# Two queues of side work in a streaming-encoder block, and all expert gate tables made beside the dense up products

## The chip, the cores and the metric

The kernel runs on one core of a Trainium2 chip, in one launch. The metric is device time in microseconds (us), the median over runs. The engines are PE (TensorE; PEld is its loading of weights), DVE (VectorE), ACT (ScalarE), POOL (GpSimd, which here issues the gathers) and SP (SyncE, which issues all other transfers). They run side by side, each in the order of its own program, and wait for each other on semaphores.

## What is computed

One layer over 1024 tokens of width 1024, in float32. What matters here:

```python
hn = rms_norm(h, norm_mix_w)
proj = hn @ w_in                                  # z, x/B/C, dt, GLU, branch gates
y_ssm = ssd_chunked_scan(...) + d_skip[:, None] * x_ssm        # 32 heads of 64
y_a = gated_group_rms_norm(y_ssm, z, ssd_norm_w) @ w_ssd_out
y_b = silu(layer_norm(causal_depthwise_conv(u, conv_dw_w))) @ w_conv_out
h = h + (sigmoid(gate_a) * y_a + sigmoid(gate_b) * y_b) @ w_o
# PEER: 8 heads, each picks 16 of 128*128 experts for each token
sv, si = lax.top_k(scores, 16)                    # of 128 keys, twice per head
best, j = lax.top_k(cand, 16)                     # of the 16*16 sums
gate = softmax(best)
act = gelu(einsum("thkd,td->thk", u_tab[expert], xb))
h = h + einsum("thk,thkd->td", gate * act, v_tab[expert])
h = h + sigmoid(rms_norm(h) @ w_ple_gate) * (p @ w_ple_proj)
return rms_norm(h, final_norm_w)
```

A token needs 128 experts; each has a row of 1024 numbers in `u_tab` (`peer_u`) and in `v_tab` (`peer_v`).

## The kernel before

The tokens are worked in two halves of 512. Each matmul in float32 is made of three in a rounded type: `weight` loads 128x1024 numbers of a weight ("a weight" below), ACT makes its high part `hl` (L156) and DVE the rest (L157), and `mm3` makes 8 x 3 matmuls of 128x512. In order the stages are glu (16 weights), gates0 (17), ssd0 (48), merge0 (32), choose0 (16), the same four again for the second half (gates1 to choose1), and then the expert layer.

The expert layer handles its tokens in two ways. The second quarter and the fourth (512 tokens) go through all 16384 experts densely: `dense_up` multiplies a weight of `peer_ut` with the tokens (128 experts, index e) and takes the GELU, `dense_down` multiplies that by the gate G of each token for each expert, and by a weight of `peer_v`. G is nearly all zeros and is built by `gate_table`: for four tokens DVE makes a one-hot tile in a `row` buffer (L734, L736), PE multiplies it (L739, "a set" below) and ACT copies it out (L742); a piece of CT tokens is then written to `DG` in DRAM. There are four tables of 128 tokens, one for each block that goes the dense way.

The first and the third quarter are gathered, in four blocks of 128 tokens numbered 0 to 3. `gather_up` fetches 128 rows of `peer_u` for each of 128 steps (`fetch`, L763: an indirect DMA of 512 KB into one of eight `row` buffers) and DVE multiplies them with the tokens and adds up (L778, "a product"). `gather_down` fetches rows of `peer_v`, four tiles for each of 32 steps ("a sum step"), and PE adds them up in `gv` (L797). Which experts a token needs comes from `choose` (the first top-k) and `choose_block` (the second), both on DVE.

The e's are split. In the stage up, the first EU = 56 of them are multiplied and `z` is parked in DRAM (`DZ`); in both, the other 72 go through up and down at once, in groups of four; in down, the 56 parked ones are read back. finish ends the layer: f1 for the dense tokens, f0 for the gathered.

Choosing, gathering, tables and the wide convolution are written as generators that give up after a bit of work and name its price. Each `weight` calls `tick`, which runs them as far as a credit goes that the stage's entry in `rates` gives:

```python
    def tick(self, anchor):
        with self.tc.issue_after(anchor.ins):
            self.cc = self.run(self.cq, self.cc + self.cr)
            self.gc = self.run(self.gq, self.gc + self.gr)
```

`cq` holds the convolution, `gq` all the rest, one after the other or woven (`weave(a, b, n)`: after each part of a, n parts of b). What an engine then does first is set by the order in which a scheduler places the recorded instructions; every engine keeps to it.

Of the kernel before, what the change touches and what calls it, by code (L numbers as in the profile page):

```python
# [8 lines left out]
F32 = mybir.dt.float32  # L9
# [12 lines left out]
S = 1024  # L22
# [7 lines left out]
CT = 16  # L30
# [6 lines left out]
for _name, _w in (("nm", 8), ("cw", 128), ("cb", 32), ("sn", 16), ("dw", 248), ("db", 8), ("lw", 8),  # L37
                  ("lb", 8), ("bo", 8), ("nf", 8), ("np", 8), ("fn", 8)):
    PCOL[_name] = (_n, _w)
    _n += _w  # L40
# [3 lines left out]
class K:  # L44
    def begin(k):
        xs = [k.xin(h) for h in range(2)]
        hn = [k.norm_in(0, xs[0])]
        with k.tc.issue_after(k.rx.ins):
            hn.append(k.norm_in(1, xs[1]))
        for j in range(2):  # L50
            k.nc.sync.dma_start(k.dsk[64 * j:64 * j + 64], k.I["dsk"][j::2].partition_broadcast(64))
        k.stage("glu")
        for i in range(8):
            k.glu_in(i, hn)
            k.cq.append(k.conv31(0, i))
        k.cq.extend([k.conv31(1, i) for i in range(8)])
        k.hn = hn[0]

    def mix(k, h):
        k.stage(f"gates{h}")  # L60
        k.ssd_dt(h)
        for i in range(16):
            k.gates_in(h, i)
        k.stage(f"ssd{h}")
        for g in range(NG):
            k.ssd_group(h, g)
        k.stage(f"merge{h}")
        if h:
            k.gq = deque([k.weave(chain(k.gate_table(0), k.gate_table(1)), chain(*k.gq), 1)])
        k.merge(h)  # L70

    def __init__(self, ctx, nc, tc, I, out):
        self.nc, self.tc, self.I, self.out = nc, tc, I, out
        self.sb = ctx.enter_context(tc.tile_pool(name="sb", bufs=1))
        self.ps = ctx.enter_context(tc.tile_pool(name="ps", bufs=1, space=PSUM))
        self.dr = ctx.enter_context(tc.tile_pool(name="dr", bufs=1, space=DRAM))
        self.scope = self.gp = None
        self.bufs = {"A": 15, "F": 8, "U": 9, "cu": 1, "ca": 1}
        self.EU, self.G4 = 56, 4
        self.cq, self.gq = deque(), deque()  # L80
        self.cc = self.gc = 0.0
# [9 lines left out]
    def run(q, credit):  # L91
        while q and credit > 0:
            try:
                credit -= next(q[0])
# [12 lines left out]
    def tick(self, anchor):  # L107
        with self.tc.issue_after(anchor.ins):
            self.cc = self.run(self.cq, self.cc + self.cr)
            self.gc = self.run(self.gq, self.gc + self.gr)  # L110

    def flush(self, q):
        self.run(q, 1e9)

    def stage(self, name):
        self.cr, self.gr = self.rates[name]


    def A(self, shape, dtype=F32, tag="A", pool=None):
        t = (pool or (self.ap if tag == "A" else self.scope)).tile(  # L120
            [128, {"cu": 544, "F": 516}.get(tag, 512)], F32, name=tag, tag=tag, bufs=self.bufs[tag])
# [79 lines left out]
    def setup(self):  # L201
# [6 lines left out]
        self.dsk = c([128, 16], "dsk")  # L208
# [230 lines left out]
    def ssd_pair(self, h, u, X, z, C, G):  # L439
# [66 lines left out]
        nc.vector.scalar_tensor_tensor(X, X, self.dsk[:, u:u + 1], pd, op0=OP.mult, op1=OP.add)  # L506
# [218 lines left out]
    def gate_table(self, i):  # L725
# [3 lines left out]
        for c in range(NC):  # L729
            st = [self.A([128, 32, CT], tag="F") for _ in range(4)]  # L730
            for q in range(CT // 4):
# [4 lines left out]
                nc.vector.tensor_tensor(oh[:, 1], oh[:, 1], wt[:, t0:t0 + 4, None].to_broadcast([128, 4, 128]), op=OP.mult)  # L736
                p = self.sp()
# [6 lines left out]
                yield 1.9  # L744
# [4 lines left out]
    def gather_setup(self, blk):  # L749
        h, b = blk  # L750
# [8 lines left out]
        blk += [ix, gt, act]  # L759
# [7 lines left out]
    def gather_up(self, blk):  # L767

        self.gather_setup(blk)
        h, b, ix, gt, act = blk  # L770
# [10 lines left out]
        nc.vector.tensor_tensor(act, act, gt, op=OP.mult)  # L781

    def gather_down(self, blk):

        h, b, ix, gt, act = blk
        nc = self.nc
        po = self.ps.tile([128, 2, 512], F32, name="gv", tag="gv", bufs=1)
        for s in range(32):
# [14 lines left out]
            yield 4.0  # L803
# [15 lines left out]

    def gather(self, h, bs):  # L820
        blks = [[h, b] for b in bs]
        for blk in blks:
            yield from self.gather_up(blk)
        for blk in blks:
            yield from self.gather_down(blk)
# [114 lines left out]
def body(nc, tc, I, out):  # L940
    with ExitStack() as ctx:
# [5 lines left out]
        with tc.tile_pool(name="mid", bufs=1) as k.scope:  # L947
            k.begin()
            for h in range(2):
# [4 lines left out]
                if h == 0:  # L954
                    k.hn = [k.split(k.load(k.Dhn[i])) for i in range(KT)]
                    bl = [[h, b] for b in range(HB)]
                    up, down = [k.gather_up(x) for x in bl], [k.gather_down(x) for x in bl]
                    k.gq.extend([cb[0], up[0], k.weave(down[0], chain(*cb[1:], up[1]), 3), down[1]])
        k.stage("up")
        with tc.tile_pool(name="up", bufs=1) as k.scope:  # L960
            bl = [[1, b] for b in range(HB)]
            up, down = [k.gather_up(x) for x in bl], [k.gather_down(x) for x in bl]
            rest = chain(*k.gq)
# [9 lines left out]
        with tc.tile_pool(name="A2", bufs=1) as k.ap, tc.tile_pool(name="end", bufs=1) as k.scope:  # L973
# [9 lines left out]
            k.flush(k.gq)  # L983
# [11 lines left out]
def layouts(x, p, norm_mix_w, w_in, conv_ssd_w, conv_ssd_b, dt_bias, a_log, d_skip, ssd_norm_w, w_ssd_out,  # L995
# [16 lines left out]
    def vec(a):  # L1012
# [10 lines left out]
        vec(norm_ple_w[0]), vec(final_norm_w)], axis=1)  # L1023
# [4 lines left out]
        "hpar": c(np.stack([A(dt_bias[0]), A(a_log[0])], axis=1)), "dsk": c(A(d_skip[0])),  # L1028
# [25 lines left out]
```

## Time and profile before

| | |
|---|---|
| median of 3 runs | 4177.55 us (4168.93 to 4183.31) |
| the profiled execution | 4178.62 us; its span from first to last instruction 4176.8 us |
| busy in the span | PE 3735.2 us (89%), DVE 3122.0 (75%), ACT 1477.6 (35%), POOL 1331.2 (32%) |
| moved by DMA | 1030.48 MB, mean 247 GB/s |
| granted TensorE clock, mean | 0.945 of full speed |

Busy times are those of one profiled execution. A matmul's end is modelled and matmuls overlap, so a busy PE need not be at its peak. POOL is counted busy while it issues a fetch; the transfer itself shows in the DMA columns, whose share is that of all 16 DMA engines. 1 MB is a million bytes.

### The profile page before, as it was taken

What the parts mean: (1) busy time and instruction counts of PE and PEld (TensorE: products, weight loads), DVE (VectorE), ACT (ScalarE), POOL (GpSimd) and SP (SyncE); (2) the same over time, 40 slices, a digit from 0 to 9 for tenths busy, and PEclk for the clock granted to TensorE, in tenths of its full rate; (3) what the DMA queues carried; (4) which work ended last, traced back from release to release, by engine and by line L of the source; (5) the groups of instructions that cost most, each with busy time, mean ns of one, the idle gap of its engine ahead of it and who ended that gap; (6) DMA issues with size and microseconds to landing.
All of it is one profiled execution on the core that took longest, in us unless ns stands there. A gap on an engine that the chain in (4) does not pass through costs nothing. (4 is left out here: it accounts for less than half of the span.)

```text
span 4176.8 us, 50925 instructions
## 1 busy us (share of the span) xinstructions
PE 3735.2 (89%) x17772; PEld 2825.4 (68%) x17772; DVE 3122.0 (75%) x5917; ACT 1477.6 (35%) x2616; POOL 1331.2 (32%) x1087
## 2 busy tenths in 40 slices
PE   7999898899974798899868988988999999899977
PEld 5887776678763476677745567777777777667646
DVE  5888888989899888789898347877855555764445
ACT  3135566343332355454412224422222222222233
POOL 0000000000266634244463430255644444433330
PEclk9999999999986899999979999999999999999988
DMA  3243234443698967689997884889999999999872
GB/s 135 89 154 109 95 109 132 152 145 111 223 334 302 331 233 265 237 297 346 320 312 262 315 297 152 281 290 311 338 327 318 314 309 312 325 334 316 302 253 81
DMA packets 479457, 1030.48 MB, mean 247 GB/s; under 512 B 177184, under 2 KB 208032, under 8 KB 479200
## 3 DMA queue, kind: packets, MB, share of 16 engines
q0 software_dynamic: 147456, 536.94, 35.7%
q1 hardware_dynamic: 331744, 490.29, 35.6%
q8 instruction: 140, 2.29, 0.2%
q14 instruction: 117, 0.96, 0.1%
HBM read 935.19 MB, written 91.88 MB: 246 GB/s over the span
## 5 line engine op out<-in xcount | busy, mean ns | idle before, releaser
L763 POOL DMA_INDIRECT row<-in_peer_u_dram,ix x512 | 699.1, 1366 | 1158.4 <-DMA ix<-Didx 410.5
L763 POOL DMA_INDIRECT row<-in_peer_v_dram,ix x512 | 625.0, 1221 | 837.2 <-PE gv L797 454.9
L173 PE MATMUL mm<-xk,hl 128*128 128x512 f32 x2000 | 811.3, 409 | 62.7 <-ACT F L363 22.8
L174 PE MATMUL mm<-xk,hl 128*128 128x512 f32 x2000 | 804.5, 404 | 9.7 <-DVE xk L165 9.7
L778 DVE SCALAR_TENSOR_TENSOR row<-row,xr 128x1024 f32<-128x1024 f32 x512 | 612.3, 1221 | 130.3 <-DMA row<-in_peer_u_dram,ix 118.1
L157 DVE TENSOR_TENSOR hl<-raw,hl 128x1024 fp32r<-128x1024 f32 x422 | 514.7, 1222 | 214.5 <-ACT hl L156 209.2
L156 ACT ACTIVATE hl<-raw 128x1024 fp32r<-128x1024 f32 x422 | 444.3, 1054 | 622.4 <-PE mm L176 288.8
L176 PE MATMUL mm<-xk,hl 128*128 128x512 f32 x2000 | 513.5, 394 | 3.4 <-DVE hl L157 3.4
L173 PEld LDWEIGHTS mm<-xk,hl 128*128 128x128 f32 x2000 | 388.5, 195 | 170.3 <-ACT F L363 27.1
L174 PEld LDWEIGHTS mm<-xk,hl 128*128 128x128 f32 x2000 | 387.2, 194 | 104.7 <-DVE xk L165 18.0
L176 PEld LDWEIGHTS mm<-xk,hl 128*128 128x128 f32 x2000 | 372.7, 188 | 85.2 <-issue 6.9
L173 PE MATMUL sp<-xk,hl 128*128 128x512 f32 x1024 | 408.7, 400 | 20.0 <-ACT xk L164 18.0
L174 PE MATMUL sp<-xk,hl 128*128 128x512 f32 x1024 | 404.3, 395 | 0.0
L310 DVE SCALAR_TENSOR_TENSOR ca<-cu,prm,ca 128x512 f32<-128x512 f32 x480 | 359.7, 749 | 35.9 <-ACT ca L308 27.7
L797 PE MATMUL gv<-row,sel 128*32 128x512 f32 x2048 | 282.1, 649 | 55.8 <-DMA row<-in_peer_v_dram,ix 47.6
L888 DVE TENSOR_TENSOR acc<-acc,sp 128x512 f32<-128x512 f32 x160 | 106.9, 685 | 224.3 <-PE sp L176 224.2
L176 PE MATMUL sp<-xk,hl 128*128 128x512 f32 x1024 | 257.6, 392 | 0.0
L173 PEld LDWEIGHTS sp<-xk,hl 128*128 128x128 f32 x1024 | 195.1, 191 | 75.3 <-ACT xk L164 19.7
L174 PEld LDWEIGHTS sp<-xk,hl 128*128 128x128 f32 x1024 | 194.8, 190 | 50.5 <-issue 10.9
L176 PEld LDWEIGHTS sp<-xk,hl 128*128 128x128 f32 x1024 | 190.9, 188 | 53.0 <-issue 13.4
L734 DVE TENSOR_TENSOR row<-io,kt 128x1024 f32<-128x1024 bf16 x128 | 152.9, 1222 | 83.3 <-PE gv L797 79.5
L164 ACT ACTIVATE zs<-A 128x512 fp32r<-128x512 f32 x128 | 78.7, 626 | 346.3 <-DVE A L877 137.2
(266 smaller groups left out, 5762.3 us busy)
## 6 DMA issues: line engine op xcount, KB each, us to landing
raw<-in_w_in_dram SPq DMA_DIRECT2D x146, 512.0 KB, 3.6
raw<-in_peer_ut_dram SPq DMA_DIRECT2D x128, 512.0 KB, 7.1
raw<-in_peer_v_dram SPq DMA_DIRECT2D x128, 512.0 KB, 7.2
DG<-F SPq DMA_DIRECT2D x128, 256.0 KB, 6.1
G<-DG SPq DMA_DIRECT2D x128, 256.0 KB, 9.8
ab<-Dac SPq DMA_DIRECT2D x32, 512.0 KB, 5.4
raw<-in_w_ssd_out_dram SPq DMA_DIRECT2D x32, 512.0 KB, 4.2
raw<-in_peer_wq_dram SPq DMA_DIRECT2D x32, 512.0 KB, 5.1
```

Source lines behind the costliest of these rows:

```text
L156: nc.scalar.activation(h, raw, AF.Copy)
L157: self.tick(nc.vector.tensor_tensor(l, raw, h.bitcast(F32), op=OP.subtract))
L164: self.nc.scalar.activation(t[:, 0], src, AF.Copy)
L173: mm(ps, w[k][0], x[:, 0], start=start and k == 0, stop=False)
L174: mm(ps, w[k][0], x[:, 1], start=False, stop=False)
L176: self.pe = mm(ps, w[k][1], x[:, 0], start=False, stop=stop and k == n - 1)
L310: nc.vector.scalar_tensor_tensor(acc, u[:, j:j + 512], self.par("dw", i * 31 + j), acc, op0=OP.mult, op1=OP.add)
L734: nc.vector.tensor_tensor(oh, self.io128[:, None, None, :].to_broadcast([128, 2, 4, 128]), kt[:, :, t0:t0 + 4, None].to_broadcast([128, 2, ...
L763: self.nc.gpsimd.indirect_dma_start(out=r, out_offset=None, in_=self.I[table], in_offset=bass.IndirectOffsetOnAxis(ap=ix[:, j, s:s + 1], a ...
L778: nc.vector.scalar_tensor_tensor(r, r, 1.0, xr, op0=OP.mult, op1=OP.mult, accum_out=act[:, j, s:s + 1])
L797: m = nc.tensor.matmul(po[32 * j:32 * j + 32, n, :], sel[:, j, s % 4, :], rows[j][:, n * 512:(n + 1) * 512], start=s == 0, stop=s == 31)
L888: nc.vector.tensor_tensor(self.acc[i], self.acc[i], p, op=OP.add)
```

## The change

There are three queues: `rq` holds the four `gather_down`, `gq` everything else, and `rates` has three numbers for each stage. A generator that has to wait for another one yields None, and the queue then stops until the next tick. gather_up of a block waits until the block before last is written out; gather_down waits for its own gather_up.

All four gate tables are made in up, with pieces of 32 tokens instead of 16, in four new buffers `S` of 128x1024 instead of the eight `F` of 128x516. G is then read in runs of 4 x 32 numbers (512 bytes) instead of 4 x 16. `yield 1.9` stands between the one-hot tile and the matmul, no longer behind the copy. EU is no longer fixed: up takes e's until `gq` is empty and their number is a multiple of four, which comes out at 88. both then has 40 e's. gq gets the gather_up of blocks 2 and 3 after up.

The skip weights `d_skip`, before loaded by two small broadcasting transfers into `dsk`, become 16 more columns `ds` of the parameter tile `prm`.

```diff
-CT = 16
+CT = 32
@@ begin
-        for j in range(2):
-            k.nc.sync.dma_start(k.dsk[64 * j:64 * j + 64], k.I["dsk"][j::2].partition_broadcast(64))
@@ mix
-        if h:
-            k.gq = deque([k.weave(chain(k.gate_table(0), k.gate_table(1)), chain(*k.gq), 1)])
@@ __init__
-        self.rates = dict(glu=(6.0, 0), gates0=(6.0, 0), ssd0=(0.5, 0), merge0=(6.4, 0), choose0=(0.85, 0),
-                          gates1=(0, 8.0), ssd1=(0.8, 4.0), merge1=(0, 6.6), choose1=(0, 5.4),
-                          up=(0, 5.6), both=(0, 3.0), down=(0, 2.6))
+        self.rates = dict(glu=(6.0, 0, 0), gates0=(6.0, 0, 0), ssd0=(0.5, 0, 0), merge0=(6.4, 0, 0),
+                          choose0=(0.85, 0, 0), gates1=(0, 4.2, 0.5), ssd1=(0, 1.7, 0.4), merge1=(0, 2.6, 0.4),
+                          choose1=(0, 0.8, 0.5), up=(0, 5.2, 0.5), both=(0, 2.4, 0.45), down=(0, 2.4, 0.45))
@@ tick
             self.gc = self.run(self.gq, self.gc + self.gr)
-
-    def flush(self, q):
-        self.run(q, 1e9)
+            self.rc = self.run(self.rq, self.rc + self.rr)
+
+    def flush(self):
+        while self.gq or self.rq:
+            self.run(self.gq, 4.0)
+            self.run(self.rq, 1.0)
@@ gate_table
-            st = [self.A([128, 32, CT], tag="F") for _ in range(4)]
+            st = [self.A([128, 32, CT], tag="S") for _ in range(4)]
@@ gather_down
-            yield 4.0
+            yield 1.0
@@ body
-                    up, down = [k.gather_up(x) for x in bl], [k.gather_down(x) for x in bl]
-                    k.gq.extend([cb[0], up[0], k.weave(down[0], chain(*cb[1:], up[1]), 3), down[1]])
+                    k.gq.extend([cb[0], k.weave(chain(*cb[1:]), k.gather_up(k.blks[0]), 1), k.gather_up(k.blks[1])])
+                    k.rq.extend([k.gather_down(x) for x in k.blks])
@@ body, up
-            k.gq = deque([cb[0], k.weave(chain(cb[2], k.gate_table(2), cb[3], k.gate_table(3)), rest, 1), cb[1]])
+            first = chain(k.gate_table(0), cb[2], k.gate_table(1), cb[3], cb[0], k.gate_table(2), cb[1], k.gate_table(3))
+            k.gq = deque([k.weave(first, chain(*k.gq), 1)])
             k.dense_in()
-            for e in range(k.EU):
+            e = 0
+            while k.gq or e % k.G4:
                 nc.sync.dma_start(k.DZ[e], k.dense_up(e))
-            k.flush(k.gq)
-            k.gq.extend([up[0], k.weave(down[0], up[1], 3), down[1]])
+                e += 1
+            k.EU = e
+            k.gq.extend([k.gather_up(x) for x in k.blks[2:]])
```

How the order of the built programs changes, counted between the weights of a stage (DVE's products, choosing units of one head and table sets, PE's sum steps):

| stage | products before / now | sum steps | choosing units | table sets |
|---|---|---|---|---|
| gates1 | 10 / 8 | 0 / 0 | 8 / 16 | 0 / 0 |
| ssd1 | 139 / 60 | 22 / 0 | 24 / 16 | 0 / 0 |
| merge1 | 40 / 69 | 10 / 3 | 0 / 0 | 54 / 0 |
| choose1 | 67 / 15 | 4 / 9 | 0 / 0 | 10 / 0 |
| up (56 / 88 weights) | 0 / 104 | 28 / 36 | 32 / 32 | 64 / 128 |
| both (144 / 80) | 231 / 137 | 32 / 18 | | |
| down (56 / 88) | 25 / 119 | 27 / 28 | | |
| finish | 0 / 0 | 5 / 34 | | |

Of the index searches of choose (two for each head, side and block), 58 stand between the weights of up before and 25 now. A fetch belongs to each product, four to each sum step.

DVE in the middle of ssd1, from one weight's low part (`hl<-raw,hl`) on, before:

```order
L157 TENSOR_TENSOR hl<-raw,hl 128x1024
L778 SCALAR_TENSOR_TENSOR row,act<-row,xr 128x1024
L482 TENSOR_TENSOR A<-A,ee 128x128
L684 CAST U<-U 128x256
L778 SCALAR_TENSOR_TENSOR row,act<-row,xr 128x1024
L675 RECIPROCAL sm<-sm 128x8
L778 SCALAR_TENSOR_TENSOR row,act<-row,xr 128x1024
L372 SCALAR_TENSOR_TENSOR F<-F,prm 128x512
L778 SCALAR_TENSOR_TENSOR row,act<-row,xr 128x1024 x3
L483 TENSOR_TENSOR A<-A,sp 128x128
L778 SCALAR_TENSOR_TENSOR row,act<-row,xr 128x1024
```

The same weight now (line numbers are four or five higher, L778 is L785):

```order
L162 TENSOR_TENSOR hl<-raw,hl 128x1024
L785 SCALAR_TENSOR_TENSOR row,act<-row,xr 128x1024
L666 MAX U<-U 128x8
L670 MAX_INDEX U<-U 128x8
L376 SCALAR_TENSOR_TENSOR F<-F,prm 128x512
L487 TENSOR_TENSOR A<-A,sp 128x128
L162 TENSOR_TENSOR hl<-raw,hl 128x1024
L785 SCALAR_TENSOR_TENSOR row,act<-row,xr 128x1024
L667 MAX_INDEX U<-U 128x8
L668 MATCH_REPLACE U<-U 128x112
L376 SCALAR_TENSOR_TENSOR F<-F,prm 128x512
```

Seven products stood between two steps of the state update (L483, now L487) and the next weight's low part was far off; now there is one product to a weight.

POOL's last fetches, before:

```order
L763 DMA row<-in_peer_v_dram,ix 128x1024 x4
L763 DMA row<-in_peer_u_dram,ix 128x1024 x3
L763 DMA row<-in_peer_v_dram,ix 128x1024 x4
L763 DMA row<-in_peer_u_dram,ix 128x1024 x35
L763 DMA row<-in_peer_v_dram,ix 128x1024 x128
L1050 UNCONDITIONAL_BRANCH
```

And now:

```order
L767 DMA row<-in_peer_u_dram,ix 128x1024 x4
L767 DMA row<-in_peer_v_dram,ix 128x1024 x4
L767 DMA row<-in_peer_u_dram,ix 128x1024 x3
L767 DMA row<-in_peer_v_dram,ix 128x1024 x144
L1055 UNCONDITIONAL_BRANCH
```

Before, the last `peer_u` fetch stood at the start of down, with 128 fetches of `peer_v` after it for the whole of down; now 144 of them stand behind the last `peer_u` fetch, whose product DVE has at the end of down.

PE near its end, around the last sum step (`gv<-row,sel`), before:

```order
L173 MATMUL mm<-vhl,hl 128x512
L174 MATMUL mm<-vhl,hl 128x512
L176 MATMUL mm<-vhl,hl 128x512
L797 MATMUL gv<-row,sel 32x512 x8
L176 MATMUL mm<-vhl,hl 128x512
L173 MATMUL mm<-xk,hl 128x512
L174 MATMUL mm<-xk,hl 128x512
```

And now (L797 is L808; L823 are the transposes that end a block, L199 sums squares for the norm of f0):

```order
L178 MATMUL mm<-vhl,hl 128x512
L179 MATMUL mm<-vhl,hl 128x512
L181 MATMUL mm<-vhl,hl 128x512 x2
L808 MATMUL gv<-row,sel 32x512 x224
L823 MATMUL gv<-ident,row 128x128 x8
L199 MATMUL sp<-A,ones 128x512
L178 MATMUL mm<-xk,hl 128x512
```

Before, the last steps stood one by one between matmuls of f1 (`mm<-xk,hl`); now 224 / 8 = 28 steps stand together, after five of the eight rounds of f1.

## Rows read from the trace of the kernel before

**Rows 1.** Busy time in windows by stage, us: span, engines (instructions), PE clock, DMA share, GB/s.

```profile
197.00:1030.00 833.00, 779.86 (x3622) 619.34 (x3621) 739.91 (x1389) 397.06 (x677) 5.81 (x51) 0.97 0.39 127
302.00:681.00 379.00, 353.66 (x1742) 281.39 (x1741) 328.27 (x539) 218.64 (x414) 5.26 (x47) 0.96 0.33 106
1030.00:2127.00 1097.00, 932.32 (x4663) 700.71 (x4662) 967.29 (x2023) 462.59 (x949) 500.07 (x370) 0.91 0.81 286
1139.00:1673.00 534.00, 414.29 (x2049) 292.65 (x2049) 474.03 (x994) 214.74 (x408) 297.41 (x223) 0.86 0.84 295
2127.00:2677.00 550.00, 465.98 (x2422) 339.74 (x2421) 362.35 (x1005) 171.96 (x404) 177.95 (x151) 0.91 0.74 265
2677.00:3596.00 919.00, 873.54 (x4010) 670.38 (x4009) 600.72 (x873) 228.98 (x295) 476.19 (x358) 0.99 0.92 315
3596.00:3970.00 374.00, 350.88 (x1663) 250.09 (x1665) 209.84 (x292) 86.01 (x114) 136.85 (x119) 0.98 0.95 321
3970.00:4177.00 207.00, 157.73 (x700) 110.52 (x692) 103.85 (x143) 76.37 (x106) 33.09 (x28) 0.89 0.48 165
```

The engines stand in the order PE, PEld, DVE, ACT, POOL. The windows are gates0 to choose0, ssd0, gates1 to choose1, ssd1, up, both, down, finish.

**Rows 2.** DVE's groups in ssd1, 1139:1673: count, busy us, mean ns, idle before.

```profile
L778 DVE SCALAR_TENSOR_TENSOR row<-row,xr 128x1024 f32<-128x1024 f32 x141 | 168.1, 1221 | 12.9 <-DMA row<-in_peer_u_dram,ix 11.4 <-DMA xr<-Dxt 0.7 <-issue 0.6
...
L778 DVE DVE_READ_ACCUMULATOR row<-row,xr 128x1 f32 x141 | 11.9, 84 | 0.0
```

**Rows 3.** PE's waits in 1139:1673: us in total, times, longest.

```profile
PE sp L489 <- DVE A L483: 35.2, 6, 11.3
```

**Rows 4.** Windows again: steady both, steady down, fastest 50 us, entry of up.

```profile
3052.00:3557.00 505.00, 497.07 (x2387) 370.41 (x2380) 283.86 (x388) 127.46 (x164) 242.00 (x198) 1.00 0.91 312
3732.00:3912.00 180.00, 177.70 (x869) 125.05 (x869) 91.00 (x122) 41.63 (x55) 64.14 (x58) 1.00 0.94 319
1125.00:1175.00 50.00, 50.00 (x224) 41.40 (x223) 43.94 (x66) 17.13 (x26) 39.61 (x28) 1.00 1.03 410
...
2127.00:2250.00 123.00, 71.61 (x320) 46.48 (x319) 119.56 (x544) 26.59 (x37) 52.12 (x44) 0.74 0.74 256
```

**Rows 5.** SP's timeline at the start: start us, us, what it issues, count.

```profile
11.28 1.47 SPq L51 DMA_DIRECT2D dsk<-in_dsk_dram  x2
12.80 16.61 SPq L152 DMA_DIRECT2D raw<-in_w_in_dram  x3
```

**Rows 6.** ACT's timeline at the start; in brackets the idle time before.

```profile
36.89 1.06 ACT L156 ACTIVATE hl<-raw 128x1024 fp32r<-128x1024 f32 x1 [14.08 <-DMA raw<-in_w_in_dram]
```

**Rows 7.** PE's matmuls of all 128 table sets, costliest groups, whole span.

```profile
L739 PE MATMUL sp<-row 128*128 128x128 f32 x1024 | 136.0, 286 | 26.0 <-DVE row L736 25.0 <-ACT F L742 0.6 <-ACT A L604 0.4
```

**Rows 8.** DMA queues in 3052:3557: packets, MB, share of 16 engines.

```profile
q0 software_dynamic: 28225, 102.78, 56.0%
q1 hardware_dynamic: 53792, 54.53, 35.0%
```

**Rows 9.** The hardware queue in up, 2127:2677.

```profile
q1 hardware_dynamic: 31211, 65.01, 32.7%
```

**Rows 10.** The page's DMA issues: count, KB each, median us to landing.

```profile
DG<-F SPq DMA_DIRECT2D x128, 256.0 KB, 6.1
```

**Rows 11.** DMA queues in steady down, 3732:3912.

```profile
q1 hardware_dynamic: 36492, 27.63, 51.4%
q0 software_dynamic: 8127, 29.62, 42.2%
```

**Rows 12.** Chain that ended last, 3985:4177: start us, us, what.

```profile
3994.91 6.06 DMA row<-in_peer_v_dram,ix
4001.01 3.63 PE gv L797 x16
...
4030.66 1.85 PE gv L797 x16
...
4090.53 1.81 PE mm L176 x8
```

**Rows 13.** POOL's timeline in finish.

```profile
3996.31 0.94 POOL L763 DMA_INDIRECT row<-in_peer_v_dram,ix  x1 [0.30 <-issue]
```

More of the change, by code (lines that the diff above doesn't have):

```diff
@@ L37 @@
 for _name, _w in (("nm", 8), ("cw", 128), ("cb", 32), ("sn", 16), ("dw", 248), ("db", 8), ("lw", 8),
[L38 removed]
+                  ("lb", 8), ("bo", 8), ("nf", 8), ("np", 8), ("fn", 8),
+                  ("ds", 16)):
     PCOL[_name] = (_n, _w)
@@ L93, in run @@
             try:
-                credit -= next(q[0])
+                c = next(q[0])
+                if c is None:
+                    return 0.0
+                credit -= c
             except StopIteration:
@@ L749, in gather_setup @@
     def gather_setup(self, blk):
-        h, b = blk
+        h, b = blk["hb"]
         nc = self.nc
@@ L758, in gather_setup @@
         act = self.gp.tile([128, 4, 32], F32, name="act", tag="act", bufs=2)
-        blk += [ix, gt, act]
+        blk.update(ix=ix, gt=gt, act=act)
     def fetch(self, table, ix, j, s):
@@ L767, in gather_up @@
     def gather_up(self, blk):
+        while blk["n"] > 1 and "out" not in self.blks[blk["n"] - 2]:
+            yield None
         self.gather_setup(blk)
-        h, b, ix, gt, act = blk
+        h, b = blk["hb"]
+        ix, gt, act = blk["ix"], blk["gt"], blk["act"]
         nc = self.nc
@@ L781, in gather_up @@
         nc.vector.tensor_tensor(act, act, gt, op=OP.mult)
+        blk["up"] = True
     def gather_down(self, blk):
-        h, b, ix, gt, act = blk
+        while "up" not in blk:
+            yield None
+        h, b = blk["hb"]
+        ix, act = blk["ix"], blk["act"]
         nc = self.nc
@@ L818, in gather_down @@
                           rs.rearrange("p (k t) -> p k t", t=128))
[L820 to L825, printed above, removed]
+        blk["out"] = True
     def resid(self, k):
@@ L955, in body @@
                     k.hn = [k.split(k.load(k.Dhn[i])) for i in range(KT)]
-                    bl = [[h, b] for b in range(HB)]
-                    up, down = [k.gather_up(x) for x in bl], [k.gather_down(x) for x in bl]
-                    k.gq.extend([cb[0], up[0], k.weave(down[0], chain(*cb[1:], up[1]), 3), down[1]])
+                    k.blks = [{"n": HB * g + b, "hb": (g, b)} for g in range(2) for b in range(HB)]
+                    k.gq.extend([cb[0], k.weave(chain(*cb[1:]), k.gather_up(k.blks[0]), 1), k.gather_up(k.blks[1])])
+                    k.rq.extend([k.gather_down(x) for x in k.blks])
         k.stage("up")
         with tc.tile_pool(name="up", bufs=1) as k.scope:
-            bl = [[1, b] for b in range(HB)]
-            up, down = [k.gather_up(x) for x in bl], [k.gather_down(x) for x in bl]
-            rest = chain(*k.gq)
-            k.gq = deque([cb[0], k.weave(chain(cb[2], k.gate_table(2), cb[3], k.gate_table(3)), rest, 1), cb[1]])
+            first = chain(k.gate_table(0), cb[2], k.gate_table(1), cb[3], cb[0], k.gate_table(2), cb[1], k.gate_table(3))
+            k.gq = deque([k.weave(first, chain(*k.gq), 1)])
             k.dense_in()
-            for e in range(k.EU):
+            e = 0
+            while k.gq or e % k.G4:
                 nc.sync.dma_start(k.DZ[e], k.dense_up(e))
-            k.flush(k.gq)
-            k.gq.extend([up[0], k.weave(down[0], up[1], 3), down[1]])
+                e += 1
+            k.EU = e
+            k.gq.extend([k.gather_up(x) for x in k.blks[2:]])
         apx.close()
```

23 lines of the change are left out of this document (11 added, 12 removed).

## The prediction

> **What bounds the kernel now.** I read the windows by stage first [rows 1]; their edges are the starts of ScalarE's copy (L156) of a stage's first weight, two or three weights ahead of TensorE. Two of them are twins: 197:1030 holds gates, ssd, merge and choose of the first half of the tokens, 1030:2127 the same stages of the second half, with the same weights. They take 833 and 1097 us; the ssd stage alone 379 and 534. The reader is to see VectorE (DVE) at 474 of 534 us there, PE at 414 with a granted clock of 0.86. What fills DVE there are 141 products with gathered rows, 168.1 us, and the reads of their sums, 11.9 [rows 2], besides the choosing of experts. PE's longest wait there is for DVE's state update [rows 3]. So the second half is bound by DVE, through work that runs ahead for later.
>
> From 2677 on PE is busy 95% and 94% of its windows, DMA 92% and 95% [rows 1]: two limits close together. In 2127:2677 PE is busy 466 of 550; its first 123 us have DVE at 119.6 and PE at 71.6 [rows 4], since choosing is finished late. At the start SP issues the skip weights at 11.28, its next three issues take 16.61 us [rows 5], and ScalarE stands 14.08 us until the first weight is there [rows 6].
>
> **The change, part by part.** The sum is made against the profiled execution's own 4178.6 us (the span and 1.8 around it), 1.1 above the median.
>
> *Skip weights.* Two loads go that fetch 4 bytes at a time. ScalarE is free at 22.81 (36.89 less 14.08), so at most 14 us come back; nothing, if the loads of x ahead hold the queue. I take 14: the slow issues begin right behind these two.
>
> *Second half relieved.* By the order (table above), ssd has 60 products instead of 139, 16 units of choosing instead of 24, no sum steps; merge and choose lose 64 table sets. DVE in ssd then has 474 − 79 × 1.30 − 11 (8 units of some 1.4, my estimate for five small operations each) = 360 us, its twin 328. I take the twin's 833, 12 sum steps more (1.85 us each [rows 12], 22 in all) and half of the 32 by which DVE has more: 871, a gain of 226. Bounds: 855 (−242) where DVE's surplus is hidden, and 896 (−201) where ssd keeps DVE's present 60 us of idle time too.
>
> *up.* It grows from 56 to 88 weights and takes all 128 table sets, 104 products and 36 sum steps. PE: 24 matmuls of 0.23 us (8 in 1.81 [rows 12]) are 5.5 per weight, 484; sets at 136.0/128 = 1.06 [rows 7], 136; steps, 67: 687 us. DMA: a fetch costs 56.0% of 505 us for 102.78 MB, or 196 fetches of 0.524 MB [rows 8], 1.44 us of all engines; 248 of them are 358. The hardware queue took 32.7% of 550 us for 65.0 MB [rows 9], 2.77 per MB; now 109 MB (weights, z, tables, 6 of others), 302. Together 660: PE is the bound by little. The same sum for before is 428 on PE, and it took 550, 122 over, 51 of them idle in the first 123 us. Fewer of choose's index searches are left over (25 instead of 58), so I take half of the 51, 25. New is a wait: a piece fills all four S buffers, so the next piece's first copy on ScalarE waits until they are written, and behind it stand the copies of the next weights and the GELUs that free sp banks. A table write landed 6.1 us after issue [rows 10] at half the size; 15 such changes are 92 us with no cover. The cover is three split weights and other sp banks; I take 28. So 740, +190; bounds 687 (+137) and 809 (+259, all 122 over again).
>
> *both.* 80 weights, 209 fetches, 18 steps. The stretch 3052:3557 moved 54.5 MB on the hardware queue, just what 80 weights and 10 G tiles are, with 198 fetches: 505 us [rows 4, 8]. Eleven fetches more (16 us of DMA) and fewer sum steps about cancel. So 505 instead of 919: −414; bounds 490 and 520.
>
> *down.* 88 weights, 231 fetches, 28 steps: PE 484 + 52 = 536. In 3732:3912 a fetch cost 42.2% of 180 us over 56.5 of them, 1.35, and the hardware queue 51.4% over 27.63 MB, or 26.4 weights with z and G, 3.51 each [rows 11]. Now 231 × 1.35 + 88 × 3.51 = 621: DMA is the bound. G rows of 512 bytes instead of 256 make this cheaper by an amount that no row shows; at 2.77 per MB all of it would be 567. I take 610, near the upper end because a share of 0.94 is what this stretch reaches with PE full [rows 4]. So +236; bounds 570 and 642 (fetches at 1.44).
>
> A rule bears on this. In bytes, down moves 213 MB, 349 GB/s over 610 us, while the steady stretch shows 319; the best 50 us show 410 [rows 4]. The Trainium skill (DMA: Bandwidth & Descriptors, Specifications) gives a limit of some 358 GB/s from HBM per core; by it down takes at least 595 us, 15 less than my term, which would make the sum 4126. The trace's 410 says that the limit is no hard one here.
>
> *The tail.* Behind the last dense matmul stand 35 sum steps, all 32 of block 3 among them and 28 in one run on PE (order above); now seven stand there, between the matmuls of finish. A step needs four fetches: at least 4 × 1.24 us on POOL (0.94 and 0.30 between [rows 13]) = 4.96. With eight row buffers two steps are under way: 4.96 + 6.06 landing + 1.85 to 3.63 on PE [rows 12], over two, is 6.4 to 7.3. The longer PE time is that behind a wait. I take 6.8: 28 × 6.8 = +190; bounds 139 and 205. PE has nothing else to do there, and what follows the last step is as before.
>
> Sum: 4178.6 − 14 − 226 + 190 − 414 + 236 + 190 = **4141 us**.
>
> **Rivals.**
> 1. *DMA has room.* Then the dense stages run at PE's pace and POOL nearly paces the tail (5.9 a step): up 700, both 490, down 570, tail +165, second half −242: 4178.6 − 14 − 242 + 150 − 429 + 196 + 165 = 4005. For it speak the 410 GB/s; against it that no long stretch [rows 1] exceeds 321.
> 2. *DMA is the limit at 320 GB/s, slower.* The fetches that the second half no longer makes (370 POOL instructions there now [rows 1], some 200 left) must go through the dense stages. up: 239 MB, 747, with the 53 of stalls 800 (+250); both 515 (−404); down 666 (+292); tail 205: 4178.6 − 14 − 226 + 250 − 404 + 292 + 205 = 4282. It decides for slower as soon as up, both and down together pass 1893 us (1843 now, plus 240 gained, less 190 in the tail). For it speak 315 and 321 GB/s at shares of 0.92 and 0.95; against it that PE was 94% busy in those windows, so that nobody asked for more.
> 3. *No change.* Tables and gathers do stand elsewhere in the order, so the change does what it says; but a tail of 205 and an up of 765 make 4181 of my own sum.
>
> **How the numbers follow.** Chances: my forecast 0.45, DMA with room 0.20, no change 0.12, slower 0.23. What a measurement of this kernel can tell from no change is about 0.3%, 12.5 us; the three runs shown lie 14 apart. Faster by more: 0.65, within: 0.12, slower by more: 0.23. The forecast's own range is 4090 to 4170; with the rivals drawn in until about 2 in 10 is left out, 4035 to 4240.
>
> **What would show it.** Start: the first weight's copy on ScalarE near 23 us. Second half: about 870 us from gates to choose, PE's wait for the state update gone, clock over 0.93. up near 740 with ScalarE waiting for DMA once per piece. down near 610 with a DMA share of 0.95 or more and PE waiting for late weights or rows. Tail: some 28 steps at 6 to 7 us on an otherwise idle PE. I am wrong if down goes below 575 (DMA had room) or above 660, if the table pieces hold up more than 60 us, or if the tail's steps take under 5.5 us.

## The result, and the profile after

The changed kernel takes 4248.8 us (median of 4 runs, 4238.41 to 4258.07), the kernel before beside it 4177.55 (median of 3 runs; one more, at 4864.99, was a slow one and is not compared). The ratio is 1.0177, its 95% interval 1.0155 to 1.02: the change made the kernel about 1.8% slower. I had forecast 4141 with a range up to 4240. The profiled execution took 4247.69 us, its span 4245.9.

The same windows by stage as [rows 1], of the kernel after: busy us (instructions) of PE, PEld, DVE, ACT, POOL, then PE clock, DMA share, GB/s. They are the first half from gates0 on, ssd0, the second half, ssd1, up, both, down, finish.

```profile
184.00:1017.00 833.00, 779.51 (x3620) 619.21 (x3619) 739.78 (x1388) 396.75 (x677) 5.81 (x51) 0.97 0.38 126
288.00:668.00 380.00, 354.41 (x1745) 282.20 (x1744) 328.48 (x539) 219.35 (x415) 5.26 (x47) 0.96 0.32 106
1017.00:1941.00 924.00, 815.80 (x3797) 633.06 (x3796) 791.42 (x1961) 401.50 (x694) 250.84 (x198) 0.93 0.65 223
1126.00:1534.00 408.00, 353.04 (x1714) 281.71 (x1713) 363.22 (x741) 211.07 (x401) 79.84 (x64) 0.92 0.54 178
1941.00:2768.00 827.00, 709.67 (x3769) 549.92 (x3768) 582.08 (x1116) 290.31 (x720) 326.93 (x254) 0.93 0.81 292
2768.00:3272.00 504.00, 488.11 (x2279) 375.61 (x2277) 342.58 (x494) 128.16 (x168) 283.62 (x213) 1.00 0.96 345
3272.00:3846.00 574.00, 543.73 (x2486) 401.52 (x2486) 418.24 (x614) 135.19 (x177) 277.08 (x220) 0.98 0.99 357
3846.00:4246.00 400.00, 238.97 (x1122) 122.03 (x1122) 110.55 (x153) 77.71 (x109) 143.37 (x140) 0.78 0.66 233
```

Against [rows 1], whose edges are found in the same way: the second half is 173 us shorter, up 277 longer, both 415 shorter, down 200 longer, finish 193 longer. In finish PE is busy 239 of 400 us at a clock of 0.78. The chain that ended last shows what it does there (start us, us, what):

```profile
3975.85 5.68 DMA row<-in_peer_v_dram,ix
3981.66 3.40 PE gv L808 x16
3988.92 5.76 DMA row<-in_peer_v_dram,ix
3994.72 3.71 PE gv L808 x16
...
4112.80 1.97 PE gv L808 x16
```

One fetch, one sum step, one fetch, one sum step: the links of the chain on PE lie some 13 us apart, and with eight row buffers two steps go by in that time. PE's timeline has the 28 steps of the one run between 3928.8 and 4114.7 us, 6.6 us each. In up, some of the waits of each engine (us in total, times, longest):

```profile
PE sp L744 <- DVE row L740: 34.0, 7, 15.4
PE gv L808 <- DMA row<-in_peer_v_dram,ix: 27.9, 13, 5.9
DVE row L738 <- PE sp L744: 70.2, 22, 6.4
DVE row L785 <- DMA row<-in_peer_u_dram,ix: 55.6, 20, 8.2
ACT S L747 <- DMA DG<-S: 54.8, 31, 5.3
POOL row L767 <- PE gv L808: 161.9, 26, 20.9
```

PE waits for one-hots, DVE for a row buffer that PE still reads or for a row that has not landed, ACT for a piece to be written, POOL for a free row. No single wait stands out; my reading, which these rows suggest and do not prove, is that each engine, in its program's order, passes its wait on. At the start ScalarE has the first weight at 22.99 us, 13.9 earlier than in [rows 6]:

```profile
22.99 1.04 ACT L161 ACTIVATE hl<-raw 128x1024 fp32r<-128x1024 f32 x1
```

### The profile page after: what moved, and what is told of

Same layout as the page of the kernel before. It is cut to its first block, busy times and chain, and to the rows that moved or that the text cites. A ratio compares the mean times of both kernels' runs of the same rounds, so it can differ in the third digit from the quotient of the medians.

```text
span 4245.9 us, 51048 instructions
## 1 busy us (share of the span) xinstructions
PE 3750.6 (88%) x17772; PEld 2835.7 (67%) x17772; DVE 3122.9 (74%) x5917; ACT 1484.3 (35%) x2616; POOL 1288.9 (30%) x1087
## 5 line engine op out<-in xcount | busy, mean ns | idle before, releaser
L767 POOL DMA_INDIRECT row<-in_peer_u_dram,ix x512 | 639.6, 1249 | 1461.1 <-DVE row L785 575.6
L767 POOL DMA_INDIRECT row<-in_peer_v_dram,ix x512 | 642.3, 1254 | 669.6 <-PE gv L808 332.2
L785 DVE SCALAR_TENSOR_TENSOR row<-row,xr 128x1024 f32<-128x1024 f32 x512 | 614.3, 1221 | 142.7 <-DMA row<-in_peer_u_dram,ix 114.5
L808 PE MATMUL gv<-row,sel 128*32 128x512 f32 x2048 | 290.6, 688 | 142.2 <-DMA row<-in_peer_v_dram,ix 142.0
L808 PEld LDWEIGHTS gv<-row,sel 128*32 128x32 f32 x2048 | 58.7, 118 | 309.2 <-issue 162.1
```

The costliest lines, as they stand in the source:

```text
L767: self.nc.gpsimd.indirect_dma_start(out=r, out_offset=None, in_=self.I[table], in_offset=bass.IndirectOffsetOnAxis(ap=ix[:, j, s:s + 1], a ...
L785: nc.vector.scalar_tensor_tensor(r, r, 1.0, xr, op0=OP.mult, op1=OP.mult, accum_out=act[:, j, s:s + 1])
L808: m = nc.tensor.matmul(po[32 * j:32 * j + 32, n, :], sel[:, j, s % 4, :], rows[j][:, n * 512:(n + 1) * 512], start=s == 0, stop=s == 31)
```

## The experiments

My first theory was that gathers and tables hold each other up in up (theory 1); its rivals were the pieces' buffers (theory 2) and DMA. Two more came up on the way: the fetches at the end (theory 3), and the distribution of all fetches (theory 4). In the diffs the left side is the changed kernel unless it says before.

**The skip weights alone**, on the kernel before: the diff's parts with `ds` and `dsk`, nothing else.

> The kernel before with nothing but the skip weights as 16 columns of the parameter tile. If the two small broadcasting loads were what held up the first weight, ScalarE copies it near 23 us instead of 36.9, all later stages keep their lengths, and the whole is 14 us (0.33%) shorter. Rival: the start is hidden by a later stage, and the time stays within 3 us.

Measured 4151.95 us, ratio 0.9956 (0.9942 to 0.997). ScalarE's first weight stands at 23.70 us, and the later stages keep their lengths within 10 us. The ratio is a gain of 12 to 24 us; the 14 lie in it, and the copy itself comes 13.2 us earlier. The term is right.

**Without gathers.** The edit, in its main lines (`...` marks what is left out); the loads that set a block up, and the way of its sum to the output, go as well.

```diff
-                r = self.fetch("peer_u", ix, j, s)
-                nc.vector.scalar_tensor_tensor(r, r, 1.0, xr, ..., accum_out=act[:, j, s:s + 1])
                 yield 1.14
@@ gather_down
-            rows = [self.fetch("peer_v", ix, j, s) for j in range(4)]
...
             yield 1.0
```

> The changed kernel without its gathers: no fetch, product or sum step (the expert sum of the gathered blocks is left out, their tokens keep the residual); the queues still count the same prices, so up still has 88 weights and all 128 table sets. It gives every stage's length without a fetch. Theory 1, fetches and products in up hold up the tables and the matmuls (shared row buffers, DVE in program order): up falls from 827 to about 675 us (484 for the weights, 136 for the sets, 25 for the entry, 28 for the pieces). Rival, theory 2, the pieces' single set of S buffers and the one-hots on DVE make up long by themselves: up stays above 740. The second half (gates to choose) falls from 924 to 835-850, near its twin's 833, both from 503 to 445, down from 574 to 490, finish from 400 to 180-190. Whole: about 3650 by theory 1, 3720 by theory 2.

Measured 3550.93 us, span 3549.1. Windows of the second half, ssd1, up, both, down, finish:

```profile
1016.00:1813.00 797.00, 764.22 (x3630) 614.00 (x3628) 614.14 (x1609) 398.69 (x691) 0.00 (x0) 0.97 0.38 126
1125.00:1469.00 344.00, 338.55 (x1734) 273.72 (x1733) 289.65 (x609) 213.17 (x407) 0.00 (x0) 0.99 0.33 109
1813.00:2451.00 638.00, 607.25 (x3177) 518.87 (x3176) 459.28 (x941) 287.02 (x718) 0.00 (x0) 0.98 0.50 174
2451.00:2895.00 444.00, 444.00 (x1961) 367.76 (x1960) 185.51 (x217) 127.02 (x164) 0.00 (x0) 1.00 0.41 130
2895.00:3361.00 466.00, 466.00 (x2056) 385.54 (x2055) 279.85 (x363) 134.00 (x176) 0.00 (x0) 1.00 0.60 188
3361.00:3549.00 188.00, 142.58 (x554) 108.99 (x552) 101.53 (x140) 75.21 (x104) 0.00 (x0) 0.86 0.27 92
```

up falls to 638 with all its table sets, with 31 us of PE idle: the tables by themselves cost no more than I took for them (673 with the entry and the pieces). The second half falls to 797, below the 833 of its twin, which carries the wide convolution. So the twin was no floor. The whole is 100 us below what theory 1 gave.

**Pieces of 16 in eight S buffers**: `CT = 16`, `"S": 8`, 512 columns each.

> The changed kernel with pieces of 16 tokens again, in eight S buffers of 128x512 (the same room): two pieces have buffers at once, and G is read in runs of 256 bytes again. Theory 2, a piece that fills all S buffers holds ScalarE up until its writes have landed: up falls by about 55 us (the 54.8 us that the copies into S wait for DMA) from 827 to 772. Theory 1: up stays within 15 us. For the read length: where DMA bounds down (its share was 0.99) down grows from 574 to 595-620 and both by 5 to 15; where PE bounds them they stay within 5.

Measured 4314.35, ratio 1.0344 (1.0317 to 1.0372). up and down:

```profile
1940.00:2754.00 814.00, 703.84 (x3770) 545.21 (x3769) 581.62 (x1117) 280.35 (x721) 329.68 (x254) 0.94 0.83 298
...
3246.00:3878.00 632.00, 553.98 (x2491) 408.26 (x2490) 423.16 (x620) 136.65 (x176) 282.91 (x226) 0.95 0.99 334
```

up falls by 13 us, not 55: theory 2 falls, for most of ACT's waits for S were not on the path. down grows by 58 at the same DMA share of 0.99, with 334 GB/s in place of 357 and six fetches more: DMA bounds down with runs of 256 bytes, and reading G in longer runs saves most of these 58 us. both does not grow (492 us, with 17 fetches fewer); finish does, by 32.

**Gathers earlier**: merge1 (5.2, 1.0), choose1 (3.0, 1.0), up (5.2, 1.0).

> The changed kernel with higher rates in merge1 (5.2, 1.0), choose1 (3.0, 1.0) and up (5.2, 1.0); ssd1 stays relieved. By its order 7 sum steps stand behind the last dense matmul instead of 34, EU comes out at 64, merge1 has 92 products and 8 steps (69 and 3), choose1 31 and 24 (15 and 9), up 65 and 32 (104 and 36). Theory 3, the steps at the end cost their full 6.9 us each because nothing lies beside them, while merge1 and choose1 have DMA to spare: finish falls by about 180 us to 220; up 670-690, both 805-815, down 430, merge1 plus choose1 +75 to +100, whole about 4165, 2% less than the changed kernel. Rival: the 20 steps and 39 products moved into merge1 and choose1 cost there what they cost at the end (+185), whole about 4260, no gain.

Measured 4289.55, ratio 1.0288 (1.0272 to 1.0303). finish falls to 223 and the second half costs only 23 more (947), but up, with 64 weights instead of 88, takes 903 us. A 50-us window near its entry, its longest waits of PE, and PE's timeline there (start, us, idle before in brackets):

```profile
2080.00:2130.00 50.00, 13.61 (x64) 2.47 (x64) 14.09 (x23) 0.00 (x0) 28.27 (x29) 0.60 0.87 297
```

```profile
PE gv L808 <- DMA row<-in_peer_v_dram,ix: 214.0, 32, 16.3
```

```profile
2083.49 3.64 PE L808 MATMUL gv<-row,sel 128*32 128x512 f32 x16 [7.02 <-DMA row<-in_peer_v_dram,ix]
```

POOL fetches as fast as rows come free, 29 in 50 us; the sum steps stand in PE's order ahead of the dense matmuls, and between 1990 and 2220 us PE does nothing else. The tail had moved, it was not gone.

**The kernel before without gathers**, the same edit.

> The kernel before without its gathers (the same expert sums left out as in the changed kernel without gathers, which took 3550.9 us). It prices everything in the change but the gathers: tables in up or half in merge1, 88 or 56 parked weights, pieces of 32 or 16, the start. Theory 4, all of the loss lies in where the gathers fall: this kernel takes 3550 + 14 (start) = 3565 us, give or take 15, and the gathers cost before 4178 - 3565 = 613 us, now 697. Rival: the tables' new place itself costs, and this kernel is below 3540 us.

Measured 3601.01, span 3599.2. Second half, ssd1, up, both, down, finish:

```profile
1030.00:1916.00 886.00, 831.05 (x4139) 676.97 (x4138) 726.82 (x1759) 460.67 (x947) 0.00 (x0) 0.96 0.40 133
1138.00:1515.00 377.00, 348.88 (x1731) 279.64 (x1730) 310.10 (x703) 212.86 (x407) 0.00 (x0) 0.95 0.30 99
1916.00:2328.00 412.00, 380.21 (x1902) 321.68 (x1901) 299.08 (x732) 168.28 (x399) 0.00 (x0) 0.96 0.48 163
2328.00:3119.00 791.00, 791.00 (x3491) 655.00 (x3490) 338.37 (x406) 227.05 (x293) 0.00 (x0) 1.00 0.45 128
3119.00:3411.00 292.00, 291.67 (x1285) 240.62 (x1284) 176.86 (x229) 84.80 (x111) 0.00 (x0) 1.00 0.65 184
3411.00:3599.00 188.00, 142.76 (x556) 109.23 (x554) 101.76 (x141) 75.20 (x104) 0.00 (x0) 0.86 0.28 92
```

That is 36 us above theory 4's figure, on the far side from the rival. All that is not gathers is 50 us cheaper in the changed kernel: 14 at the start, 36 by the tables, the choosing and the way they are spread. It loses in the gathers alone: 697 us (4245.9 less 3549.1) against 578 (4176.8 less 3599.2).

**The rates of before in the second half**: gates1 8.0, ssd1 4.0, merge1 6.6, choose1 5.4.

> The changed kernel with the rates of before in the second half (8.0, 4.0, 6.6, 5.4, and 0.5 for the sum steps): its ssd1 has 200 products and 14 steps (60 and none), EU comes out at 64, 7 steps stand in the tail. By the cost of a fetch in each stage of the changed kernel (stage less the same stage without gathers, over its fetches: second half 0.65 us, up 0.74, both 0.28, down 0.49, finish 1.53) the second half takes 797 + 0.65 x 412 = 1064, up 508 + 98 = 606, both 800, down 422, finish 207: with the 1017 ahead about 4115 us, 1.5% below before. Rival, what the run with gathers earlier showed: more sum steps than fetches have landed stand in TensorE's order at the entry of up, up then takes over 750 and the whole over 4230.

Measured 4182.96, ratio 1.0016 (0.9999 to 1.0032). finish is 216 and up 608, as forecast, but ssd1 takes 589 us with DVE 527 busy, and the second half 1138. Neither account held.

**One-hots in two buffers of their own**, pieces of 16 in four S.

> The changed kernel with pieces of 16 in four S buffers of 128x512, and the one-hot tiles in two buffers of their own in place of the eight row buffers that they share with the gathers. Against the kernel with pieces of 16 in eight S buffers (up 813, whole 4314). Theory 1, gathers and tables hold each other up through the shared row buffers: up falls to 740-770. Rival: the fetches cost what they cost through DMA and program order, and up stays within 15 us of 813. down about 630 in both.

Measured 4267.67, ratio 1.0224 (1.0207 to 1.0241). up is 793 against 814: 21 us, between the two accounts, although S went from eight buffers back to four as well. Shared row buffers are a part of it (theory 1), not the whole cause.

**Tables 0 and 1 back in merge1 and choose1**, in pieces of 16 in the `F` buffers, with the higher rates of before for `gq` in these two stages.

> The changed kernel with tables 0 and 1 back in merge1 and choose1, pieces of 16 in the F buffers, as before; the two queues, the low rate in ssd1 and the skip weights stay. EU comes out at 48, 27 steps stand in the tail (28 now). So it has the relieved second half and the tail of the changed kernel with the tables of before. Theory 4, the tables' place is neutral and the gathers' distribution is the loss: second half 924 + 68 = 992, up 490, both 995, down 323, finish 390, whole 4205, still above before. Rival, the tables' place is the loss: the whole is under 4165.

Measured 4273.18, ratio 1.0249 (1.0229 to 1.0268), no faster than the changed kernel. Second half 997, up 556, both 1002, down 325, finish 366, the last with 117 fetches. The rival falls: even less the 65 us by which the run with pieces of 16 in eight S buffers is above the changed kernel, this is 4208, and its bound was 4165. So the tables' place is not the loss. up was 66 us dearer than I had worked out, and why is open.

**Gathers spread over more stages**, two sets of rates.

> The changed kernel with rates that put the gathers into more stages: gates1 (8.0, 0.5), ssd1 (2.4, 0.4), merge1 (3.0, 0.4), choose1 (0.4, 0.3), up (6.0, 0.8). By its order ssd1 has 146 products and 7 steps, merge1 70 and 10, choose1 20 and 8, up 12 and 39, EU comes out at 56, both has 253 and 27, two steps stand in the tail. Theory 4, the loss lies in the fetches at the end: by the fetch costs of the runs so far (ssd1 0.7 to 1.0 us each, merge1 0.6, choose1 0.5, up 0.8, both 0.26, down 0.55, tail 1.53) the gathers cost 560 us over the 3563 of the same stages without them, 4125 us in all, 1.2% below before. Rival, as in the run with gathers earlier: steps whose rows have not landed stand ahead of the matmuls at the entry of up, up has over 150 us of idle TensorE and the whole is over 4200.

> The same idea with lower rates: gates1 (6.0, 0.5), ssd1 (2.4, 0.2), merge1 (4.0, 0.2), choose1 (0.2, 0.1), up (5.2, 0.6). ssd1 has 116 products and one step, merge1 95 and 5, choose1 20 and 3, up 17 and 40, EU comes out at 68, 18 steps stand in the tail. Theory 4: the tail is 110 us where the run beside it has 12, the rest about equal, 4175 us in all, 50 above the run beside it. Rival, the stage that relieves ssd1 most wins whatever the tail: below the run beside it.

Measured 4181.83, ratio 1.0034 (1.0018 to 1.0051), and 4201.7, ratio 1.0099 (1.0064 to 1.0133). Of the first, ssd1 and finish:

```profile
1126.00:1660.00 534.00, 373.11 (x1813) 288.47 (x1811) 465.09 (x916) 214.68 (x405) 230.15 (x173) 0.85 0.72 248
...
3983.00:4176.00 193.00, 150.52 (x656) 108.21 (x648) 102.93 (x142) 76.31 (x106) 16.07 (x16) 0.90 0.41 146
```

The tail is gone (193 us), and some 60 us of the loss with it (1.0034 against 1.0177), but not the 124 that I expected: in ssd1 173 fetches cost 190 us over the 344 without, 1.1 each. The second has a longer tail (290) and a shorter ssd1 (478), and is 20 us slower, not 50: theory 4 has the sign right and its costs per fetch too low. Its down:

```profile
3456.00:3900.00 444.00, 425.16 (x2028) 304.62 (x2027) 291.11 (x415) 105.99 (x140) 209.92 (x173) 1.00 0.99 361
```

Down here moves 361 GB/s over 444 us, all DMA engines taken.

**No transfers**: products and steps stay, fetches go.

```diff
-                r = self.fetch("peer_u", ix, j, s)
-                nc.vector.scalar_tensor_tensor(r, r, 1.0, xr, ...
+                r = self.row()
+                nc.vector.scalar_tensor_tensor(r, xr, 1.0, xr, ...
@@ gather_down
-            rows = [self.fetch("peer_v", ix, j, s) for j in range(4)]
-                                         rows[j][:, n * 512:(n + 1) * 512], ...
+                                         sel.rearrange("p a b c -> p (a b c)"), ...
```

> The changed kernel with all products and sum steps but without the fetches: products read the tokens' own tile twice, steps read the selection tile in place of the rows (the gathered sums are left out of the result). DVE and TensorE do the gathers' work, and nothing is transferred for them or waited for. Without gathers the kernel took 3551, with them 4248: 697 us. If the transfers and the waits for them make most of that, this run is near 3551 + 237 (128 steps of 1.85 on TensorE) + 20 to 60 = 3810 to 3850. If it is DVE's time and program order, it is over 3950.

Measured 3989.68, span 3987.9. Second half, ssd1, up, both, down, finish:

```profile
1016.00:1934.00 918.00, 812.27 (x3795) 630.26 (x3795) 791.07 (x1961) 401.24 (x695) 0.00 (x0) 0.93 0.33 112
1124.00:1541.00 417.00, 355.39 (x1743) 282.08 (x1743) 366.55 (x807) 211.58 (x405) 0.00 (x0) 0.92 0.28 94
1934.00:2683.00 749.00, 696.29 (x3781) 538.90 (x3780) 575.00 (x1111) 287.49 (x719) 0.00 (x0) 0.97 0.42 148
2683.00:3202.00 519.00, 513.68 (x2396) 379.69 (x2395) 378.35 (x565) 131.25 (x167) 0.00 (x0) 0.99 0.37 119
3202.00:3778.00 576.00, 560.45 (x2662) 404.65 (x2661) 382.61 (x550) 135.12 (x179) 0.00 (x0) 0.99 0.50 156
3778.00:3988.00 210.00, 168.55 (x818) 116.49 (x816) 105.40 (x145) 76.22 (x106) 0.00 (x0) 0.89 0.25 85
```

More of it is engine work, with the waits that the program's order makes, than I had thought: 439 us. The second half takes 918 without a single fetch, 924 with them. finish falls from 400 to 210, but not by the transfers alone: the order changed too, and finish has 264 of the sum steps' matmul records here, 592 in the changed kernel (17 and 37 steps). A run of steps here (start us, us), and the window of the changed kernel's run of 28 (`gv` alone, PE, PEld, DVE, ACT):

```profile
3799.60 21.64 PE L807 MATMUL gv<-sel 128*32 128x512 f32 x200
```

```profile
3928.00:4115.00 187.00, 86.57 (x448) 15.69 (x448) 0.00 (x0) 0.21 (x1) 0.68 0.86 301
```

With no rows to wait for a step takes 1.73 us (21.64 over 200/16), so 28 would take 48: of the 186 us of that run some 140 are transfers and waits for them.

**The kernel before without transfers**, the same edit.

> The kernel before with all products and sum steps and without the fetches (the gathered sums are left out of the result), as in the changed kernel without transfers, where engine work was 439 us (3990 less 3551) and transfers with the waits for them 258 (4248 less 3990). Without gathers the kernel before took 3601. If the changed kernel loses through its tail, where each fetch is waited for, engine work is the same 439 here: 4040 us, and the transfers cost 138, some 120 less than in the changed kernel. Rival, the changed order makes the engines' own work dearer: this run is at or below 3950 and the transfers cost over 220 here too.

Measured 4108.1, span 4106.3. Second half, ssd1, up, both, down, finish:

```profile
1032.00:2118.00 1086.00, 933.31 (x4699) 703.01 (x4697) 985.70 (x2076) 466.70 (x953) 0.00 (x0) 0.93 0.33 112
1157.00:1650.00 493.00, 394.81 (x2011) 282.44 (x2009) 443.79 (x975) 218.30 (x414) 0.00 (x0) 0.89 0.25 83
2118.00:2614.00 496.00, 440.38 (x2382) 330.24 (x2383) 341.13 (x952) 169.47 (x400) 0.00 (x0) 0.93 0.39 134
2614.00:3557.00 943.00, 885.26 (x4061) 678.46 (x4060) 632.38 (x934) 232.04 (x297) 0.00 (x0) 0.97 0.39 114
3557.00:3920.00 363.00, 363.00 (x1760) 253.71 (x1759) 180.44 (x235) 86.11 (x114) 0.00 (x0) 1.00 0.53 149
3920.00:4106.00 186.00, 140.27 (x552) 108.06 (x550) 101.88 (x141) 75.10 (x104) 0.00 (x0) 0.87 0.27 92
```

It is 68 us above my expectation, on the far side from the rival: engine work was 507 us before (now 439), and transfers cost only 70 (now 258).

**The fastest version**: the kernel before, skip weights as parameters, and one-hots in three buffers of their own in up.

> The kernel before with the skip weights as parameters (4152 us, 0.9956 of before) and, in up alone, one-hot tiles in three buffers of their own in place of the shared row buffers; up has 64 table sets and 28 sum steps there. By the 20 us that the same edit took off the changed kernel's up at 128 sets, up falls by 8 to 12 us from 556 and the whole to about 4142, 0.993 of before. Rival: nothing that can be measured, since up waits for choosing there; 0.995 to 0.997.

Measured 4144.06, ratio 0.9915 (0.9901 to 0.9928). up is 528 us; in the run with the skip weights alone it was 557. Of these 29 us the whole keeps some 17 (0.9915 against 0.9956). That is more than I expected in up; why is open.

## Why the prediction was wrong

The four runs without gathers and without transfers divide each stage: gathers are the stage less the same without gathers, transfers (with the waits for them) the stage less the same without transfers. Fetches are POOL's count in the windows. Each of the four was executed once. The runs without transfers are ordered anew and place sum steps elsewhere: of the changed kernel's 37 steps in finish 20 moved, most of them into both and down (hence the negative entries there, and a finish that is too high). The totals hold; single entries are good to some 20 us, those of finish now to some 40.

| us | fetches before / now | gathers | transfers alone | gathers per fetch |
|---|---|---|---|---|
| second half | 370 / 198 | 211 / 127 | 11 / 6 | 0.57 / 0.64 |
| up | 151 / 254 | 138 / 189 | 54 / 78 | 0.91 / 0.74 |
| both | 358 / 213 | 128 / 60 | -24 / -15 | 0.36 / 0.28 |
| down | 119 / 220 | 82 / 108 | 11 / -2 | 0.69 / 0.49 |
| finish | 28 / 140 | 19 / 212 | 21 / 190 | 0.68 / 1.51 |

By the spans the change is: without gathers −50, engine work of the gathers −68 (507 to 439), transfers +187 (70 to 258), together +69. Most of the +187 is the tail: the table has +169 in finish, the run of 28 steps by itself some 140. The second half gave up 172 fetches, both and down 44; up took 103 and the tail 112. They left places where a fetch costs 0.3 to 0.7 us, and more than half of them went to one where it costs 1.5, with nothing beside it.

The forecast had the tail's 190 in it. The 106 us by which it missed are up (+87), the second half (+53), the tail (+3) and both (−1), less down (−36), whose error hid a part of the others by luck.

Point by point:

- **Skip weights**, −14: −13.9, and shown by themselves.
- **The tail**, +190: +193. The mechanism was right: 28 steps at 6.6 us, where I had 6.8. Without transfers finish is 22 over the run without gathers, with 17 of the 37 steps still in it.
- **both**, −414: −415.
- **down**, +236: +200, near my lower bound (570) and rival 1's value. The run with G in runs of 256 bytes shows where my size was off: the longer runs save most of 58 us, and I had taken the upper end. DMA is not far above the engines there: without transfers, and with 12 sum steps more, down takes 576. It moved 357 GB/s over 574 us at a share of 0.99. The Trainium skill (DMA: Bandwidth & Descriptors, Specifications) puts a core's limit from HBM near 358 GB/s; these 357, and 361 over 444 us in the second spread run, lie near it for a whole stage. It was no hard limit: the first 150 us of that second down moved 368. That this limit is what held down is not shown. The same section asks for 512 bytes and more for line rate: the 334 and 357 GB/s at one share are in keeping with that.
- **up**, +190: +277, beyond my upper bound of 809. This is the step that failed: "So 740". PE's own terms held (607 us busy without gathers, I had 620 for weights and sets), and without gathers the 53 us of stalls, 28 of them for the pieces, were enough: 638, where weights, sets and stalls made 673. What failed is the price of the gathers. Products and steps alone add 111 us to the 638, where I had 67 for steps and nothing for products, and transfers with the waits for rows add 78, where I had nothing because DMA's total (660) was below PE's (687): −35 + 44 + 78 = +87. Of the waits that I tested, the pieces' buffers are worth 13 us and buffers of their own for the one-hots 21; which waits make the rest is open. My reading is that two totals near each other do not hide each other when every engine waits in its program's order.
- **Second half**, −226: −173. The other failing step: "I take the twin's 833". The twin is not what is left when gathers go (797 is), and the gathers that stay are not half hidden: they cost 127 us, where I had 38 over the twin (22 for steps, 16 for DVE's surplus): −36 + 89 = +53. In ssd1 DVE's added work shows almost one for one: DVE rises from 310 to 474 us before and from 290 to 363 now, the stage from 377 to 534 and from 344 to 408. PE loses this as idle time and as clock (0.99 without gathers, 0.92 now, 0.86 in [rows 1]). The runs without transfers show that rows were not what was waited for in ssd1 now (417 against 408); before they were in part (493 against 534). But ssd1 is the smaller part of the miss: it came out at 408, where the twin and the 16 make 395. The other 40 us are in the stages around it, where I had 22 for steps and nothing for products. merge0 in the kernel before, merge1 now, and merge1 without gathers:

```profile
681.00:917.00 236.00, 212.69 (x914) 163.51 (x913) 215.71 (x318) 103.90 (x155) 0.20 (x1) 0.95 0.46 154
1534.00:1808.00 274.00, 230.76 (x980) 174.53 (x979) 214.83 (x341) 107.48 (x169) 102.10 (x73) 0.90 0.77 274
1469.00:1700.00 231.00, 214.86 (x931) 167.92 (x930) 133.56 (x194) 103.42 (x162) 0.00 (x0) 0.94 0.45 150
```

merge1 now has the DVE time of its twin (215 us) and takes 38 us longer: DVE's busy time does not say what a product costs there.

- **Rivals.** Rival 2 had the side and the point of decision: up, both and down came to 1905 us, past the 1893 that it names. Its mechanism was not the one: DMA is the limit in down at most, which came out shorter than forecast, and of up's excess the larger part is waits (78), the rest engine work (44). Rival 1 was right on down alone. Rival 3 named up and the tail, but up passed its 765 too.

Without the tail the change does not win either: the four runs that shorten it come to between 4182 and 4290 us. In three of them ssd1 charges 1.0 to 1.1 us for each fetch that it takes (over its 344 without), up charges 0.7 to 0.9 in the table, and more where steps pile up at its entry. both is the cheap place, and takes 4.9 to 5.3 fetches for each e (358 for 72, 213 for 40, 395 for 80), where down takes 2.1 to 2.5. Parking more e's shortens the place where fetches are cheap. What stays open is whether some order keeps the 50 us of the tables and the 68 of engine work without the tail; I found none. Whether more than eight row buffers would shorten the tail was not tried.

## What to carry to other kernels

Price moved side work by the stage that receives it: run the kernel once without that work and once with its engine work but no transfers, and each stage's two differences say what a unit costs there, which neither a busy share nor a total does. Count what the other order moved between stages before you read a single difference, as the tail here shows. Work that is made cheaper early but not finished by the end of its cover comes back at full latency; count what stands behind the last covering instruction first. A twin stage with other filler is not a floor.

## What the hardware showed that I had not expected

A sum step's sixteen matmul records take 1.85 us in busy stretches and 3.64 us at up's entry in the run with gathers earlier, where PE had waited 7 to 16 us before each and the granted clock of the window was 0.60, so mostly at 1.2 instead of 2.4 GHz: a step behind such a wait took twice as long. All DMA engines were taken for 0.99 of down at 357 GB/s with G in runs of 512 bytes and at 334 with runs of 256. A DMA share of 0.99 is thus no measure of bytes.
